# Seven products for eight in three more matrix products of a two-layer decoder trunk, with the middle of each layer reordered

## The chip, the cores and the metric

The kernel runs on one core of one Trainium2 chip. The metric is the device time of one execution in microseconds (us), the median of the runs taken. The program is one launch; the weights stay in HBM and stream through the core once per execution.

## The reference

Two layers over 256 tokens with a model width of 2048, all in f32. Each layer computes, in this order:

```
h = rmsnorm(x);  proj = h @ w_in      # columns: GLU pair, q, k, v, forget logits, gates A and B (2048 each)
y_conv = silu(layernorm(causal_depthwise_conv31(a * sigmoid(gate)))) @ w_conv_out
y_attn = forgetting_attention(q, k, v, cumsum(log_sigmoid(f))) @ w_attn_out     # 8 heads of 128
x += (sigmoid(g_A) * y_conv + sigmoid(g_B) * y_attn) @ w_out
x += (silu(gate) * up) @ w_down       # [gate | up] = rmsnorm(x) @ w_gate_up, hidden width 5632
x += sigmoid(rmsnorm(x) @ w_ple_gate) * (p[i] @ w_ple_proj)
```

At the end comes one more rmsnorm, which is the output.

## The kernel before, in words

Tokens sit in two blocks of 128. A product is done in chunks of 512 output columns: two PSUM banks, one for each token block, collect 16 tiles of 128 contraction rows. f32 exactness comes from splitting both operands into a high part (fp32r) and a rest, so that every (token block, row tile) pair costs three matmuls of 128x512 (L175 to L177): high by high, high by rest, rest by high. A chunk of 2048 rows is 96 of them.

Weights arrive as *raw* tiles of two row tiles by 512 columns (512 KB, L134, issued on SyncE's queue, 7 buffers in the pool `raws`). `split` (L137) makes the high part on ScalarE (L140) and the rest on VectorE (L141), into 4 buffers each (`whs`, `wls`); one split feeds 12 matmuls. Token operands are transposed on TensorE (L295, 8 transposes per 512 channels), evacuated by ScalarE, and the rest is subtracted on VectorE (`halves`, L279); they live in a pool of 23 buffers called `pairs`.

`fast_chunks` (L211) computes two chunks together. The first 4 row tiles by two token blocks by the two weight chunks are a 2x2 by 2x2 block product, done with seven block products for eight (a Winograd form): seven products of 6 matmuls, and 12 ordinary raw tiles (`go`) of 12 matmuls for the other 12 row tiles. For it VectorE adds weights (L241: one tile `sum`, three in place on `raw`), ScalarE copies one partial product out of PSUM (L254) and VectorE combines the rest (L255 to L258, L268 to L272). The seven products split seven tiles where the ordinary way splits four. Class `Fast` (L304) makes the token side: `take` evacuates the transposed first four tiles with the gains (L314) into two f32 tiles, `make` forms four more by subtracting (L320), and splits all eight (L329, L330). In this kernel its two f32 tiles are taken from `raws`. Only the FFN's gate and up products use `fast_chunks`, from their second pair of chunks on: ten pairs per layer.

Three lists steer what goes between chunks: `turns` (transposes of finished operands), `tasks` (attention, one step for each `run`), and `background` (the depthwise convolution's 248 VectorE steps and the layer norm after it, `fill(CONV)` with a credit of 7). `chunk` calls `run` and `fill` once per four row tiles. The framework then places each engine's instructions in an order that it plans from the order of the program and from which buffers are free; on the chip each engine works through its own list in that order.

In a layer the order is: GLU chunks (4), values (2), keys and queries (4, attention begins), gates A (4, the rest of the attention), gates B alternating with the attention's output product (`attended`, L786), the convolution's output product (L814) with the merge, the output projection `wOut` (L826), FFN in three parts, and the embeddings' gate `wPG` (L875) with the projection `wPP` (L866). `Norm(g_ffn, fast=True)` (L824) is the one norm per layer with a `Fast`; its `turn(0)` runs in the second chunk of `wOut`.

Of the kernel before, what the change touches and what calls it, by code (L numbers as in the profile page):

```python
# [10 lines left out]
F32 = mybir.dt.float32  # L11
# [5 lines left out]
P = 128  # L17
D = 2048
S = 256
# [25 lines left out]
def trunk(ctx, tc, xT, xR, pT, wI, wF, wC, wA, wOut, wGU, wD, wPG, wPP, vec, bF, gF, out):  # L45
# [162 lines left out]

    def fast_chunks(fast, w1, w2, xs, ks):  # L211


        nk = 4 * len(ks)
# [6 lines left out]
                for half in range(2):  # L221
                    left.append((w[1 + g][:, half * 1024 : (half + 1) * 1024], sums, k0 + 2 * half))

        def go(n=1):
            for _ in range(n):
                if left:
                    src, sums, k0 = left.popleft()
                    parts = split(fetch(src))
                    await_x(xs, (k0, k0 + 1))
                    plain(sums, xs, k0, parts)  # L230
                    if len(left) % 2 == 0:
                        run()
                        fill(CONV)

        def product(to, which, raw):
            h, l = split(raw)
# [36 lines left out]
        return (u1, u4), (u3, u5)  # L273

    def by_four(w, n=N4):
        return [(w[g], range(4 * g, 4 * g + 4)) for g in range(n)]
# [27 lines left out]
    class Fast:  # L304


        def __init__(self):
            self.f = [raws.tile([P, 4, 2, P], F32, tag="raw", name=f"fast{next(uid)}") for _ in range(2)]

        def take(self, half, pt, gains):  # L310
            src = pt.rearrange("p k (b s) -> p b k s", b=2)
            to = self.f[0][:, 2 * half : 2 * half + 2]
            for kk in range(2):
                act.activation(to[:, :, kk, :], src[:, :, kk, :], AF.Copy, scale=gains[kk])  # L314
            if half == 1:
                self.make()

# [27 lines left out]
                    lambda b, j=j, kk=kk: self.l[0][:, 2 * j + b, kk, :],  # L345
                )

    def operand(xs, k0, src):
        for half, pt in turned(src):
            o = pair(F32R)  # L350
            halves(o, pt)
            for kk in range(2):
                xs[k0 + 2 * half + kk] = by_blocks(o[:, kk, :])

    class Norm:

# [89 lines left out]
    def hook():  # L446
        load_x(0, 2, 4)
        take(0)

    def rest(q):  # L450
        def go():
            take(q)
            if q < 3:
                load_x(q + 1)
                turns.append(rest(q + 1))
            else:
                for b in range(2):
                    nc.sync.dma_start(xt[:, b, :], xR[:, b, :])
                nc.sync.dma_start(vecs[:, KD:], vec[:, KD:])
                nc.sync.dma_start(bfs, bF.rearrange("l h -> (l h)").partition_broadcast(P))  # L460
                for n in range(N4):
                    norm.squares(n)
                norm.finish()
        return go

    for i in range(L):
# [70 lines left out]

        def logits():
            pf = bank_ms()
            for k in range(KD):  # L540
                pe.matmul(
                    pf[:16, :], lhsT=wfc[:, k].rearrange("p a h -> p (a h)"), rhs=norm.tiles[k],
                    start=(k == 0), stop=(k == KD - 1),
                )
            act.activation(fls[:16, :], pf[:16, :], AF.Copy)

        def log_forget():
# [221 lines left out]

        background.append(lazy(conv_norm))  # L770

        gate_a, y_att = [], []

        def sigmoids(c):
            pp = project(c)
            t = pair()
            for b in range(2):
                act.activation(t[:, b, :], pp[b], AF.Sigmoid, scale=norm.r(b))
            return t

        for n in range(N4):
            gate_a.append(sigmoids(GATE_A + n))
        while tasks:
            run()

        def attended(n):  # L786
            return chunk(by_four(wA[i, n], 2), o_att, bank_mm)
# [5 lines left out]
        for n in range(N4 - 1):  # L793
            t = sigmoids(GATE_B + n)
            gated_by(t, attended(n))
            y_att.append(t)
        pp = attended(N4 - 1)
        t = pair()
        for b in range(2):
            act.activation(t[:, b, :], pp[b], AF.Copy)  # L800
        s = project(GATE_B + N4 - 1)
        for b in range(2):
            g = tmp()
            act.activation(g, s[b], AF.Sigmoid, scale=norm.r(b))
            dve.tensor_tensor(t[:, b, :], t[:, b, :], g, op=ALU.mult)
        y_att.append(t)
        while background:
            fill(9)


        merged = {}
        for n in range(N4):
            t = gate_a[n]
            gated_by(t, chunk(by_four(wC[i, n], 2), o_conv, bank_mm))  # L814
            for b in range(2):
                dve.tensor_tensor(t[:, b, :], t[:, b, :], y_att[n][:, b, :], op=ALU.add)
            turns.append(lambda n=n, t=t: operand(merged, 4 * n, lambda b: t[:, b, :]))

        def residual(n, acc):
            for b in range(2):  # L820
# [1 line left out]
                dve.tensor_tensor(xc, xc, acc[b], op=ALU.add)  # L822

        norm = Norm(g_ffn, fast=True)  # L824
        for n in range(N4):
            residual(n, chunk(by_four(wOut[i, n]), merged, bank_mm))  # L826
            advance(norm, n)


        after = Norm(g_ple)  # L830
        c0 = 0
        for part, nch in enumerate(FFN_PARTS):
            hid = {}
            for c in range(c0, c0 + nch):
                w1, w2 = wGU[i, 2 * c], wGU[i, 2 * c + 1]
                if c == 0:
                    g, t = [chunk(by_four(w), norm.xs, bank_mm) for w in (w1, w2)]
                    o = [tmp() for _ in range(2)]
                else:
                    g, t = fast_chunks(norm.fast, w1, w2, norm.xs, (4, 8, 12))  # L840
                    o = t
                for b in range(2):
                    z = tmp()
                    act.activation(z, g[b], AF.Sigmoid, scale=norm.r(b))
                    dve.scalar_tensor_tensor(z, g[b], norm.r(b), z, op0=ALU.mult, op1=ALU.mult)
                    dve.scalar_tensor_tensor(o[b], t[b], norm.r(b), z, op0=ALU.mult, op1=ALU.mult)
                turns.append(lambda c=c, o=o, hid=hid: operand(hid, 4 * c, lambda b: o[b]))
            for n in range(N4):
                groups = [(wD[i, n, c], range(4 * c, 4 * c + 4)) for c in range(c0, c0 + nch)]
                residual(n, chunk(groups, hid, bank_mm))  # L850
                if part == len(FFN_PARTS) - 1:
                    advance(after, n)
# [9 lines left out]

        last = i == L - 1

        def embed(n):
            return chunk([(wPP[i, n], range(2))], ps, bank_ms)  # L866
# [6 lines left out]
        for n in range(N4):  # L873
            e = embed(n)
            acc = chunk(by_four(wPG[i, n]), norm.xs, bank_mm)  # L875
            for b in range(2):
                t = tmp()
                act.activation(t, acc[b], AF.Sigmoid, scale=norm.r(b))
                dve.tensor_tensor(t, t, e[b], op=ALU.mult)
                xc = xt[:, b, n * 512 : (n + 1) * 512]  # L880
                dve.tensor_tensor(xc, xc, t, op=ALU.add)
            if not last:
                advance(after, n)
                continue
            after.squares(n)
            if n == N4 - 1:
                after.finish()
            for b in range(2):
                xc = xt[:, b, n * 512 : (n + 1) * 512]
                dve.tensor_tensor(xc, xc, gb[n // 2][:, (n % 2) * 512 : (n % 2 + 1) * 512], op=ALU.mult)  # L890
        norm = after


# [66 lines left out]
```

## Time and profile before

| | |
|---|---|
| median of 3 runs | 2891.67 us (2891.22 to 2892.88) |
| the profiled execution | 2891.74 us |
| its span in the trace | 2889.9 us |
| TensorE matmul busy | 2855.0 us, 12884 instructions |
| VectorE busy | 2001.4 us |
| ScalarE busy | 1431.1 us |
| mean granted TensorE clock | 0.996 |
| DMA | 543.27 MB, 188 GB/s |

Times in the trace run from the span's start. Busy time of TensorE is modelled from pipelined matmuls: one matmul lasts 390 ns in the records and the next begins 0.23 us after it, so work done is better read from how many matmuls a stretch holds. A wait is put down to what ended last before it.

### The profile page before, as it was taken

How to read it: one execution, taken by the hardware profiler on the slowest of the kernel's cores; microseconds unless marked ns; L12 is line 12 of the kernel's file. 1: busy time of each engine (PE TensorE's matmuls, PEld its weight loads, DVE VectorE, ACT ScalarE, POOL GpSimd, SP SyncE). 2: the span in 40 equal slices, each digit the busy share in tenths (PEclk: the TensorE clock that was granted, in tenths of full speed). 3: DMA queues.
4: the chain of work that ended last, by engine and by line, in shares of the span. 5: the costliest groups of instructions: out<-in, count | busy, mean ns of one | idle time of the engine just before them, and what ended most of it. 6: DMA issues, size and time to landing. Idle time of an engine off the chain costs nothing.

```text
span 2889.9 us, 34305 instructions
## 1 busy us (share of the span) xinstructions
PE 2855.0 (99%) x12884; PEld 2361.8 (82%) x12884; DVE 2001.4 (69%) x2568; ACT 1431.1 (50%) x1726; POOL 9.5 (0%) x40
## 2 busy tenths in 40 slices
PE   8999999999999999999999999999999999999998
PEld 6888888788888888888888888887888888888886
DVE  5997745557678758865569966455585886688554
ACT  5445744455445435545554456444454554455444
POOL 0000000000000000000000000000000000000000
PEclk9999999999999999999999999999999999999999
DMA  7554455455556556555555544554455555556553
GB/s 279 180 179 166 166 197 191 165 185 180 207 183 209 198 178 211 182 204 189 183 176 188 180 163 175 195 190 162 177 191 207 182 196 204 181 197 211 186 203 122
DMA packets 149496, 543.27 MB, mean 188 GB/s; under 512 B 16849, under 2 KB 17105, under 8 KB 149073
## 3 DMA queue, kind: packets, MB, share of 16 engines
q1 hardware_dynamic: 149328, 541.07, 54.1%
q8 instruction: 101, 1.65, 0.2%
q14 instruction: 67, 0.54, 0.1%
HBM read 538.91 MB, written 2.10 MB: 187 GB/s over the span
## 4 chain that ended last, share of the span: by engine, by line
PE 94%; DVE 4%; DMA 1%; ACT 0%; issue 0%; SPq 0%; POOL 0%; ACTq 0%; POOLq 0%; DVEq 0%
PE mm L176 29%; PE mm L177 29%; PE mm L175 29%; PE ms L295 2%; DVE wl L141 2%; DVE pair L490 2%; PE ms L177 2%; PE ms L176 2%; PE ms L175 2%; DMA xt<-in_xR_dram 0%; PE ms L649 0%; DMA raw<-in_wI_dram 0%; PE ms L685 0%; ACT tmp L368 0%; PE ms L651 0%
## 5 line engine op out<-in xcount | busy, mean ns | idle before, releaser
L141 DVE TENSOR_TENSOR wl<-raw,wh 128x1024 fp32r<-128x1024 f32 x1054 | 1282.3, 1223 | 802.1 <-ACT wh L140 793.8
L140 ACT ACTIVATE wh<-raw 128x1024 fp32r<-128x1024 f32 x1054 | 1116.3, 1060 | 1299.9 <-PE mm L177 1186.1
L175 PE MATMUL mm<-wh,pair 128*128 128x512 f32 x3832 | 1502.8, 392 | 18.6 <-ACT wh L140 11.1
L176 PE MATMUL mm<-wl,pair 128*128 128x512 f32 x3832 | 1495.7, 390 | 1.8 <-DVE wl L141 1.8
L177 PE MATMUL mm<-wh,pair 128*128 128x512 f32 x3832 | 1495.9, 390 | 0.0
L175 PEld LDWEIGHTS mm<-wh,pair 128*128 128x128 f32 x3832 | 721.1, 188 | 166.9 <-ACT wh L140 12.0
L176 PEld LDWEIGHTS mm<-wl,pair 128*128 128x128 f32 x3832 | 721.8, 188 | 151.7 <-DVE wl L141 3.4
L177 PEld LDWEIGHTS mm<-wh,pair 128*128 128x128 f32 x3832 | 721.4, 188 | 150.7
L490 DVE SCALAR_TENSOR_TENSOR pair<-pair,vecs,pair 128x256 f32<-128x256 f32 x480 | 201.3, 476 | 0.0
L177 PE MATMUL ms<-wh,pair 128*128 128x512 f32 x192 | 74.7, 389 | 0.0
L175 PE MATMUL ms<-wh,pair 128*128 128x512 f32 x192 | 74.7, 389 | 0.0
L176 PE MATMUL ms<-wl,pair 128*128 128x512 f32 x192 | 74.7, 389 | 0.0
L241 DVE TENSOR_TENSOR raw<-raw,raw 128x1024 f32<-128x1024 f32 x60 | 73.2, 1221 | 0.9
L283 DVE TENSOR_TENSOR pair<-ms,pair 128x512 fp32r<-128x512 f32 (+1 forms) x76 | 45.1, 625 | 1.6 <-ACT pair L282 1.3
L822 DVE TENSOR_TENSOR xt<-xt,mm 128x512 f32<-128x512 f32 x64 | 41.1, 680 | 4.9 <-PE mm L177 4.9
L175 PEld LDWEIGHTS ms<-wh,pair 128*128 128x128 f32 x192 | 36.0, 188 | 7.5
L176 PEld LDWEIGHTS ms<-wl,pair 128*128 128x128 f32 x192 | 36.0, 188 | 7.5
L177 PEld LDWEIGHTS ms<-wh,pair 128*128 128x128 f32 x192 | 36.0, 188 | 7.5
L368 ACT ACTIVATE tmp<-xt 128x512 f32<-128x512 f32 x56 | 34.6, 619 | 14.9 <-DVE xt L822 8.8
L282 ACT ACTIVATE pair<-ms 128x512 fp32r<-128x512 f32 (+1 forms) x76 | 38.0, 541 | 0.6 <-PE ms L686 0.6
L285 ACT ACTIVATE pair<-ms,vecs 128x256 fp32r<-128x256 f32 x72 | 30.6, 467 | 14.4 <-DVE pair L286 14.4
L140 ACT ACTIVATE wh<-sum 128x1024 fp32r<-128x1024 f32 x20 | 21.2, 1062 | 31.3 <-PE mm L177 31.3
(167 smaller groups left out, 925.3 us busy)
## 6 DMA issues: line engine op xcount, KB each, us to landing
raw<-in_wGU_dram SPq DMA_DIRECT2D x352, 512.0 KB, 4.1
raw<-in_wI_dram SPq DMA_DIRECT2D x287, 512.0 KB, 3.8
raw<-in_wD_dram SPq DMA_DIRECT2D x176, 512.0 KB, 3.7
raw<-in_wOut_dram SPq DMA_DIRECT2D x64, 512.0 KB, 3.7
raw<-in_wPG_dram SPq DMA_DIRECT2D x64, 512.0 KB, 3.6
raw<-in_wA_dram SPq DMA_DIRECT2D x32, 512.0 KB, 4.2
raw<-in_wC_dram SPq DMA_DIRECT2D x32, 512.0 KB, 4.3
raw<-in_wPP_dram SPq DMA_DIRECT2D x8, 512.0 KB, 3.2
```

The source lines that it names most:

```text
L140: act.activation(h, raw, AF.Copy)
L141: dve.tensor_tensor(l, raw, h.bitcast(F32), op=ALU.subtract)
L175: pe.matmul(self.t, lhsT=xh, rhs=wh, start=start, stop=False)
L176: pe.matmul(self.t, lhsT=xh, rhs=wl, start=False, stop=False)
L177: pe.matmul(self.t, lhsT=xl, rhs=wh, start=False, stop=self.left == 0)
L241: add = lambda o, a, b: dve.tensor_tensor(o, a, b, op=ALU.add)
L282: act.activation(hi, src, AF.Copy)
L283: dve.tensor_tensor(lo, src, hi.bitcast(F32), op=ALU.subtract)
L295: pe.transpose(pt[:, kk * S + b * P : kk * S + (b + 1) * P], src(b)[:, c : c + P], ident)
L368: act.activation(tmp(), xt[:, b, n * 512 : (n + 1) * 512], AF.Square, accum_out=self.ss[:, b * 4 + n : b * 4 + n + 1],)
L490: dve.scalar_tensor_tensor(cv[c], u[c][:, j : j + S], w, cv[c], op0=ALU.mult, op1=ALU.add,)
L822: dve.tensor_tensor(xc, xc, acc[b], op=ALU.add)
```

## The change

`fast_chunks` also computes the gates A and B (two pairs of chunks each per layer), the output projection (two pairs) and the embeddings' gate (two pairs). It gets a callback `first` for the first chunk's result, called half-way, and may write into given tiles (`to`). Gates B are all computed first, then the attention's output product, then a pair of gates A, two chunks of the convolution's output product, and the same once more. `Fast` takes its f32 tiles from `pairs`; there is one for the merged operand, one for each norm ahead of the embeddings and of layer 2, and one made from the first layer's input (`early`). In `go`, `run` is called after every raw tile but one, and the background credit of 7 is dealt in 3 and 4.

```diff
-    def fast_chunks(fast, w1, w2, xs, ks):
+    def fast_chunks(fast, w1, w2, xs, ks, first, to=None):
...
-        def go(n=1):
+        def go(n=1, quiet=False):
...
                     plain(sums, xs, k0, parts)
-                    if len(left) % 2 == 0:
+                    fill(CONV // 2 + len(left) % 2)
+                    if not quiet:
                         run()
-                        fill(CONV)
...
         product(q5, M1, a21)
-        go()
+        go(quiet=True)
         product(q7, T3, s3)
...
-        u1, u3, u4, u5 = (tmp() for _ in range(4))
+        u1, u4, u3, u5 = [tmp() for _ in range(4)] if to is None else to
...
         add(u4, u4, c12.t)
+        first((u1, u4))
         go(2 * len(ks))
...
-            self.f = [raws.tile([P, 4, 2, P], F32, tag="raw", name=f"fast{next(uid)}") for _ in range(2)]
+            self.f = [pair().rearrange("p a (n k s) -> p (a n) k s", n=2, k=2) for _ in range(2)]
...
+            if gains is None:
+                act.activation(to, src, AF.Copy)
...
+    def early():
+        norm.fast = Fast()
+        for j in range(2):
+            norm.fast.take(
+                j, xin[0][:, j, :].rearrange("p (k s) -> p k s", k=2), [norm.gain(2 * j + kk) for kk in range(2)]
+            )
+        norm.xs.update(enumerate(norm.fast.column_tiles()))
...
-            for k in range(KD):
...
+            for k in range(4, KD):
+                pe.matmul(pf[:16, :], lhsT=lhsT(k), rhs=norm.tiles[k], start=(k == 4), stop=False)
+            for k, (hi, lo) in enumerate(norm.fast.both()):
+                pe.matmul(pf[:16, :S], lhsT=lhsT(k), rhs=hi, start=False, stop=False)
+                pe.matmul(pf[:16, S:], lhsT=lhsT(k), rhs=lo, start=False, stop=(k == 3))
...
         def sigmoids(c):
-            pp = project(c)
...
+            t = [pair() for _ in range(2)]
+            def gate(t):
+                for b in range(2):
+                    act.activation(t[b], t[b], AF.Sigmoid, scale=norm.r(b))
+            gate(fast_chunks(
+                norm.fast, wI[i, c], wI[i, c + 1], norm.xs, (4, 8, 12), gate,
+                [t[m][:, b, :] for m in range(2) for b in range(2)],
+            ))
             return t
...
+        y_att = sigmoids(GATE_B) + sigmoids(GATE_B + 2)
         while tasks:
             run()
...
+        for n in range(N4):
+            gated_by(y_att[n], chunk(by_four(wA[i, n], 2), o_att, bank_mm))
...
         merged = {}
+        fast_merged = Fast()
         for n in range(N4):
-            t = gate_a[n]
+            if n % 2 == 0:
+                gate_a = sigmoids(GATE_A + n)
...
+            t = gate_a[n % 2]
             gated_by(t, chunk(by_four(wC[i, n], 2), o_conv, bank_mm))
...
+                lambda n=n, t=t: operand(merged, 4 * n, lambda b: t[:, b, :], fast_merged if n == 0 else None)
...
-            residual(n, chunk(by_four(wOut[i, n]), merged, bank_mm))
-            advance(norm, n)
...
+        for n in range(0, N4, 2):
+            onto_x(norm, n + 1)(
+                fast_chunks(fast_merged, wOut[i, n], wOut[i, n + 1], merged, (4, 8, 12), onto_x(norm, n))
+            )
...
-        after = Norm(g_ple)
+        after = Norm(g_ple, fast=True)
...
-        after = Norm(0 if last else (i + 1) * NV)
-        for n in range(N4):
-            e = embed(n)
-            acc = chunk(by_four(wPG[i, n]), norm.xs, bank_mm)
...
+        after = Norm(0 if last else (i + 1) * NV, fast=not last)
...
+        for n in range(0, N4, 2):
+            for m in range(2):
+                e.append(pair())
+                for b, t in enumerate(chunk([(wPP[i, n + m], range(2))], ps, bank_ms)):
+                    act.activation(e[n + m][:, b, :], t, AF.Copy)
+            embedded(n + 1)(
+                fast_chunks(norm.fast, wPG[i, n], wPG[i, n + 1], norm.xs, (4, 8, 12), embedded(n))
+            )
```

In the FFN the gate's silu moves into the callback, half-way through a pair; the sum for x in `embedded` is the residual, the square sums and, in the first layer, the next norm's `turn`.

## Rows read from the trace of the kernel before

**Rows 1.** The page's first part: busy us (share of the span) xinstructions.
```profile
PE 2855.0 (99%) x12884; PEld 2361.8 (82%) x12884; DVE 2001.4 (69%) x2568; ACT 1431.1 (50%) x1726; POOL 9.5 (0%) x40
```

**Rows 2.** The chain that ended last, share of the span by engine.
```profile
PE 94%; DVE 4%; DMA 1%; ACT 0%; issue 0%; SPq 0%; POOL 0%; ACTq 0%; POOLq 0%; DVEq 0%
```

**Rows 3.** Waits of TensorE: us in total, times, longest us.
```profile
PE mm L175 <- ACT wh L140: 11.1, 3, 4.4
PE mm L175 <- ACT wh L159: 7.5, 2, 6.8
PE mm L176 <- DVE wl L141: 1.8, 3, 0.8
```

**Rows 4.** Windows: a plain chunk of `wOut`, then two FFN pairs, one set of transposes each.
```profile
core 0: us, PE busy (x) PEld busy (x) DVE busy (x) ACT busy (x) POOL busy (x), PEclk, DMA share, GB/s
586.99:609.64 22.65, 22.65 (x106) 18.85 (x105) 12.66 (x14) 11.30 (x16) 0.00 (x0) 1.00 0.53 186
1136.08:1179.16 43.08, 43.08 (x196) 35.74 (x195) 35.72 (x38) 22.76 (x24) 0.00 (x0) 1.00 0.57 195
```

**Rows 5.** The chain by time: one set of transposes between two chunks of `wOut`.
```profile
586.99 0.87 PE ms L295 x8
```

**Rows 6.** Windows around the second chunk of `wOut`, layers 1 and 2, and within the latter.
```profile
555.00:575.00 20.00, 14.89 (x63) 11.82 (x62) 11.35 (x13) 10.65 (x13) 0.00 (x0) 0.91 0.58 193
1985.00:2005.00 20.00, 15.38 (x59) 11.85 (x57) 10.39 (x12) 9.59 (x12) 0.00 (x0) 0.83 0.49 167
1995.00:2000.00 5.00, 4.76 (x12) 3.63 (x12) 3.75 (x4) 1.73 (x2) 0.00 (x0) 0.50 0.81 261
```

**Rows 7.** ScalarE's instructions in time there, layer 1: start, us, what, idle before.
```profile
546.47 1.06 ACT L140 ACTIVATE wh<-raw 128x1024 fp32r<-128x1024 f32 x1 [1.66 <-PE mm L177]
...
557.79 1.57 ACT L314 ACTIVATE fast<-ms,vecs 128x256 f32<-128x256 f32 x4 [4.44 <-PE ms L295]
559.40 2.19 ACT L329 ACTIVATE pair<-fast 128x1024 fp32r<-128x1024 f32 x2
561.49 3.88 ACT L140 ACTIVATE wh<-raw 128x1024 fp32r<-128x1024 f32 x4
```

**Rows 8.** SyncE's weight transfers there, in time.
```profile
528.89 0.33 SPq L134 DMA_DIRECT2D raw<-in_wOut_dram  x1
537.05 0.33 SPq L134 DMA_DIRECT2D raw<-in_wOut_dram  x1
...
548.82 0.33 SPq L134 DMA_DIRECT2D raw<-in_wOut_dram  x1
561.74 0.33 SPq L134 DMA_DIRECT2D raw<-in_wOut_dram  x1
```

**Rows 9.** Groups by line, engine and form: xcount | busy us, mean ns | idle before.
```profile
L141 DVE TENSOR_TENSOR wl<-raw,wh 128x1024 fp32r<-128x1024 f32 x1054 | 1282.3, 1223 | 802.1 <-ACT wh L140 793.8 <-DMA wf<-in_wF_dram 1.5 <-DMA raw<-in_wI_dram 0.7
L241 DVE TENSOR_TENSOR raw<-raw,raw 128x1024 f32<-128x1024 f32 x60 | 73.2, 1221 | 0.9
L255 DVE TENSOR_TENSOR tmp<-tmp,ms 128x512 f32<-128x512 f32 x20 | 13.6, 680 | 0.0
L541 PE MATMUL ms<-pair,wfc 128*16 128x512 f32 x32 | 7.9, 399 | 0.0
L656 PE MATMUL ms<-chs,nsel 128*128 128x256 f32 x16 | 4.5, 279 | 0.0
```

**Rows 10.** Windows: convolution under keys and queries; gates A with attention; the second GLU chunk.
```profile
180.00:240.00 60.00, 59.94 (x290) 49.93 (x289) 60.00 (x126) 29.55 (x43) 0.00 (x0) 1.00 0.49 174
252.00:348.00 96.00, 95.73 (x455) 79.64 (x455) 64.28 (x123) 64.19 (x100) 0.70 (x1) 1.00 0.44 154
...
40.00:60.00 20.00, 20.00 (x90) 16.57 (x89) 9.94 (x9) 9.34 (x10) 0.00 (x0) 1.00 0.68 231
```

**Rows 11.** The end of the trace: the last matmul, and VectorE's first instruction behind it.
```profile
2875.98 0.39 PE L177 MATMUL mm<-wh,pair 128*128 128x512 f32 x1
2876.45 1.37 DVE L879 TENSOR_TENSOR tmp<-tmp,ms 128x512 f32<-128x512 f32 x2 [8.60 <-ACT tmp L878]
```

More of the change, by code (lines that the diff above doesn't have):

```diff
@@ L346, in column_tiles, with both, operand @@
                 )
-    def operand(xs, k0, src):
+        def both(self):
+            for k in range(4):
+                j, kk = divmod(k, 2)
+                yield self.h[0][:, 2 * j : 2 * j + 2, kk, :], self.l[0][:, 2 * j : 2 * j + 2, kk, :]
+    def operand(xs, k0, src, fast=None):
         for half, pt in turned(src):
+            if fast is not None:
+                fast.take(half, pt)
+                continue
             o = pair(F32R)
@@ L353, in operand @@
                 xs[k0 + 2 * half + kk] = by_blocks(o[:, kk, :])
+        if fast is not None:
+            xs.update(zip(range(k0, k0 + 4), fast.column_tiles()))
     class Norm:
@@ L456, in go @@
             else:
+                turns.append(early)
                 for b in range(2):
@@ L539, in logits @@
             pf = bank_ms()
-            for k in range(KD):
[L541 to L544, printed above, removed]
+            lhsT = lambda k: wfc[:, k].rearrange("p a h -> p (a h)")
+            for k in range(4, KD):
[3 more added lines that the diff above has]
+                pe.matmul(pf[:16, S:], lhsT=lhsT(k), rhs=lo, start=False, stop=(k == 3))
             act.activation(fls[:16, :], pf[:16, :], AF.Copy)
@@ L791, in gated_by @@
                 dve.tensor_tensor(t[:, b, :], t[:, b, :], pp[b], op=ALU.mult)
[L793 to L808, printed above, removed]
+        y_att = sigmoids(GATE_B) + sigmoids(GATE_B + 2)
+        while tasks:
+            run()
+        for n in range(N4):
+            gated_by(y_att[n], chunk(by_four(wA[i, n], 2), o_att, bank_mm))
         merged = {}
+        fast_merged = Fast()
         for n in range(N4):
-            t = gate_a[n]
+            if n % 2 == 0:
+                gate_a = sigmoids(GATE_A + n)
+            if n == 0:
+                while background:
+                    fill(9)
+            t = gate_a[n % 2]
             gated_by(t, chunk(by_four(wC[i, n], 2), o_conv, bank_mm))
@@ L816, in trunk @@
                 dve.tensor_tensor(t[:, b, :], t[:, b, :], y_att[n][:, b, :], op=ALU.add)
-            turns.append(lambda n=n, t=t: operand(merged, 4 * n, lambda b: t[:, b, :]))
+            turns.append(
+                lambda n=n, t=t: operand(merged, 4 * n, lambda b: t[:, b, :], fast_merged if n == 0 else None)
+            )
         def residual(n, acc):
@@ L824, in trunk, with onto_x, go @@
         norm = Norm(g_ffn, fast=True)
-        for n in range(N4):
-            residual(n, chunk(by_four(wOut[i, n]), merged, bank_mm))
-            advance(norm, n)
-        after = Norm(g_ple)
+        def onto_x(norm, n):
+            def go(y):
+                residual(n, y)
+                if norm is not None:
+                    advance(norm, n)
+            return go
+        for n in range(0, N4, 2):
[3 more added lines that the diff above has]
+        after = Norm(g_ple, fast=True)
         c0 = 0
@@ L835, in trunk, with gate @@
                 w1, w2 = wGU[i, 2 * c], wGU[i, 2 * c + 1]
+                z = [tmp() for _ in range(2)]
+                def gate(g, z=z):
+                    for b in range(2):
+                        act.activation(z[b], g[b], AF.Sigmoid, scale=norm.r(b))
+                        dve.scalar_tensor_tensor(z[b], g[b], norm.r(b), z[b], op0=ALU.mult, op1=ALU.mult)
                 if c == 0:
[L837 to L841 removed]
+                    gate(chunk(by_four(w1), norm.xs, bank_mm))
+                    up = chunk(by_four(w2), norm.xs, bank_mm)
+                else:
+                    up = fast_chunks(norm.fast, w1, w2, norm.xs, (4, 8, 12), gate)
                 for b in range(2):
[L843 to L846, printed above, removed]
+                    dve.scalar_tensor_tensor(z[b], up[b], norm.r(b), z[b], op0=ALU.mult, op1=ALU.mult)
+                o = z
                 turns.append(lambda c=c, o=o, hid=hid: operand(hid, 4 * c, lambda b: o[b]))
@@ L849, in trunk @@
                 groups = [(wD[i, n, c], range(4 * c, 4 * c + 4)) for c in range(c0, c0 + nch)]
-                residual(n, chunk(groups, hid, bank_mm))
-                if part == len(FFN_PARTS) - 1:
-                    advance(after, n)
+                onto_x(after if part == len(FFN_PARTS) - 1 else None, n)(chunk(groups, hid, bank_mm))
             c0 += nch
@@ L863, in trunk @@
         last = i == L - 1
-        def embed(n):
-            return chunk([(wPP[i, n], range(2))], ps, bank_ms)
         if last:
@@ L871, in trunk, with embedded, go @@
                 nc.sync.dma_start(gb[n], gF[n * 1024 : (n + 1) * 1024].partition_broadcast(P))
-        after = Norm(0 if last else (i + 1) * NV)
-        for n in range(N4):
-            e = embed(n)
-            acc = chunk(by_four(wPG[i, n]), norm.xs, bank_mm)
[L876 to L890, printed above, removed]
+        after = Norm(0 if last else (i + 1) * NV, fast=not last)
+        e = []
+        def embedded(n):
+            def go(y):
+                for b in range(2):
+                    act.activation(y[b], y[b], AF.Sigmoid, scale=norm.r(b))
+                    dve.tensor_tensor(y[b], y[b], e[n][:, b, :], op=ALU.mult)
+                residual(n, y)
+                if not last:
+                    advance(after, n)
+                    return
+                after.squares(n)
+                if n == N4 - 1:
+                    after.finish()
+                for b in range(2):
+                    xc = xt[:, b, n * 512 : (n + 1) * 512]
+                    dve.tensor_tensor(xc, xc, gb[n // 2][:, (n % 2) * 512 : (n % 2 + 1) * 512], op=ALU.mult)
+            return go
+        for n in range(0, N4, 2):
[5 more added lines that the diff above has]
+                fast_chunks(norm.fast, wPG[i, n], wPG[i, n + 1], norm.xs, (4, 8, 12), embedded(n))
+            )
         norm = after
```

18 lines of the change are left out of this document (5 added, 13 removed).

## The prediction

> **What bounds the kernel now.** I read the page first: TensorE is busy 2855.0 of 2889.9 us, VectorE 2001.4 and ScalarE 1431.1 [rows 1]. The chain of waits agrees: 94% of it is TensorE, 4% VectorE, 1% DMA [rows 2]. The reader is to see that nothing but TensorE's own work sets the time in most stages, so that a matmul less is time less as long as its operands come in time. Then TensorE's waits, to see where they don't: it waits for the high part of a weight split three times (11.1 us, longest 4.4), for the very first weights (7.5), and for the rest part 1.8 us [rows 3]. The windows around these waits come last; two of the three stand in the second chunk of `wOut`, one in each layer [rows 6].
>
> **The price of a pair, and what goes.** A plain chunk of `wOut` takes 22.65 us between two sets of transposes, an FFN pair in the seven-product form 43.08 [rows 4]; a set of 8 transposes is 0.87 [rows 5]. So a plain pair is 2 x (22.65 - 0.87) = 43.56, a fast pair 43.08 - 0.87 = 42.21, and the form saves 1.35 us. The count says the same: 192 matmuls become 12 x 12 + 7 x 6 = 186, and six at 21.78/96 = 0.227 are 1.36. There are 4 + 2 + 2 new pairs per layer and two layers, so 16 x 1.35 = 21.6 us go from TensorE, which is the path.
>
> The TensorE page of the Trainium skill ("TensorE: Matmul & The Clock Gate", Back-to-back issue gap) gives about 131 ns as the sustained spacing of such matmuls in a real kernel and 216 ns in isolation. By the first the 96 matmuls would be an estimated 12.6 us, by the second 20.7; the 0.227 us here lies beside the second, and no stretch of this trace shows the first.
>
> **The stall in `wOut`.** SyncE issues a weight transfer about every 2.7 us (3.6 across transposes), but none between 528.89 and 537.05, and then none between 548.82 and 561.74 [rows 8]. The first gap is as wide as two buffers: the `Fast` tiles of the coming norm have taken two of the seven `raws`. ScalarE makes its last split at 546.47, then stands for 4.44 us at the evacuation of the transposes (L314), makes the operand (2.19), and only then does four splits in one go [rows 7]: with five buffers the planned order put those splits behind the operand, though the weights had long been there. TensorE ran dry meanwhile, and came back at a lower clock (0.50 granted in the 5 us from 1995) [rows 6]. The price: the window from 555 holds 63 records, 8 of them transposes, so 55 x 0.227 + 0.87 = 13.4 us of work in 20, 6.6 lost; that from 1985 holds 59, so 12.4 of work, 7.6 lost. Together 14.2; idle time alone would be 5.1 + 4.6 = 9.7. I take 14.2, since the lower clock is lost work too. The change takes the `Fast` tiles from `pairs`, so all seven buffers serve the weights, and I expect the splits to be planned ahead as in the other chunks. If they aren't, 14.2 stay. After these two, no TensorE wait of over a microsecond is left beyond the start.
>
> **What is added on VectorE and ScalarE.** A fast pair has 3 more splits (1.223 each), 4 additions (1.221) and 8 half-size combinations (0.680) on VectorE [rows 9]: 3.67 + 4.88 + 5.44 = 14.0 us per pair; ScalarE gets 3 splits and a copy, under 4 us against a load of half its time [rows 1]. The FFN pairs show the result where little else runs: 35.72 us of VectorE in 43.08, with TensorE never idle [rows 4]. In `wOut` and the embeddings' gate the residual (4 x 0.680), the gating and the next operand stand in place of the silu; 19 splits, 4 additions and 16 to 24 steps of 0.680 or less are 39 to 45 us, with two splits of `wPP` in the embeddings' pair 47, against 43 and 49 of TensorE (24 matmuls of `wPP`, 5.4 us). So these are covered: cost nothing, and if a pair's cover went, up to 2 us each.
>
> The tight place is the first two pairs, gates B, under which the rest of the attention and the convolution's layer norm run. The stage that they replace, four plain chunks, has 64.28 us of VectorE in 96.00 [rows 10]. With 2 x 14.0 it is 92.3 against 96.0 - 2.7 = 93.3 of TensorE. The credit per pair falls from 56 to 42, so the eight closing steps of the layer norm (four VectorE operations each, half as wide as the 0.680 ones) slide under the attention's output product, where plain chunks leave VectorE nearly half free (12.66 of 22.65) [rows 4]; that leaves between 92.3 and 92.3 - 32 x 0.68 = 70.5. Full load alone does no harm: under keys and queries VectorE is busy 60.00 of 60 and TensorE still 59.94 [rows 10], because four split buffers let it run up to 4 x 2.72 = 10.9 us ahead. But a pair's first half is heavier: 11 splits, 4 additions and 4 combinations are 21.0 us against 90 matmuls, 20.4. I put 1.2 us of new waits in each layer, 2.5 in all; the bounds are 0 (the 59.94) and 18 (third rival). That gates A come later, after the attention, costs nothing by itself: their weights come through the same queue in the same number (16 transfers per pair), and the only thing that waits for them is the convolution's merge, which moved behind them too.
>
> Both ends of the small terms. Logits: 16 wide matmuls become 12 wide and 8 of half width; half width lasts 279 ns against 399 [rows 9], so between nothing (half the price) and +0.9 per layer (full price); I take 0.25, 0.5 in all, nearer the first because columns set the pace. `early` puts 4 evacuations, 2 splits and 6 VectorE steps, about 4 us on each engine, beside a plain chunk in which both are half idle (9.34 and 9.94 of 20) [rows 10]: nothing, or 4 if they fall ahead of a split. Could it win? Only if it moved the start's 7.5 us wait, which it comes after. The end: behind the last matmul VectorE now first subtracts (0.68) before the sigmoid, where ScalarE read PSUM directly; the second block's subtraction runs under it. The chain behind 2875.98 [rows 11] grows by 0.7 to 1.4; I take 0.8. Silu at half-way in the FFN moves work off the pair's end, where nothing waited: 0. The doubled pace of `run` halves the gap between a head's scores and its transposes from four splits' matmuls to two (5.4 us); the softmax between must fit into that, and what it lacks is in the 2.5.
>
> **Sum**, against the profiled execution's own 2891.74 (span 2889.9 and 1.84 around it; the median of the runs is 2891.67, 0.07 away): 2891.74 - 21.6 - 14.2 + 2.5 + 0.5 + 0.8 = 2859.7. I forecast **2860**; with every addition at nothing 2856, and some 2 less if `early` eases the start; with 8 us of waits in place of 2.5, 2866.
>
> **Rivals.**
> *The stall stays in `wOut` (2874).* 2860 + 14.2, if the evacuation itself and not the buffers holds the splits back. For it: ScalarE does wait there for TensorE's transposes. Against it: the other turns, with seven buffers, show no such wait, and the gap at 528.89 has no other cause in the program.
>
> *VectorE sets the pace in gates B (2878).* With no lead left, the first half of such a pair needs 21.0 us of its own and 0.26 per us for the stage's other VectorE work ((64.28 - 32 splits of 1.223)/96) [rows 9, 10]. TensorE takes 20.4 x 96/87.1 = 22.5 us for it with the attention's matmuls (87.1 are four plain chunks). So VectorE lacks 21.0 + 5.9 - 22.5 = 4.4 us; four such pairs in the program are 18. It decides where VectorE enters a pair with less than 4.4 us of lead. The lead of up to 10.9 speaks against it.
>
> *Slower: every new `Fast` brings the stall with it (2910).* If the long hold of ScalarE is the cause (4.44 of waiting, 1.57 and 2.19 of work [rows 7]), then each `Fast` fed by transposes costs it. There will be seven: two for the merged operand, two ahead of the FFN, two ahead of the embeddings, one ahead of layer 2. At 7.1 each they cost 49.7 where two cost 14.2 now: 2860 + 49.7. The kernel is slower once one costs over (2891.7 - 2860)/7 = 4.5 us. For it: the hold of 8.2 us is three quarters of what four split buffers cover; against it: splits can be planned ahead of the hold, which needs only raw buffers.
>
> The same page of the Trainium skill (Architectural detail) says that ScalarE and VectorE queues are strict first-in first-out, so a waiting evacuation holds every split behind it. The trace agrees: four splits start together at 561.49. That rule speaks for the two rivals with the hold, and is why I leave them more than a remnant.
>
> **Chances.** Forecast 0.58 (2853 to 2868), stall stays 0.15, gates B bound 0.15, slower 0.12. About 0.2% (5.8 us) is what a measurement of this kernel can tell. The first two are faster by more; gates B bound is so in three parts of five, the rest within 0.2%: faster 0.82, same 0.06, slower 0.12. The range 2853 to 2882 holds the first two and the better part of the third, 0.8.
>
> **What would show it.** Right: 96 fewer wide matmuls (11,976 in place of 12,072); fast pairs of 42.2 us plus transposes in all new places; in `wOut` no gap of SyncE over 6 us, no burst of four splits behind L329, and a granted clock of 1.00. Wrong: TensorE waits for the rest part (VectorE) inside the gates B pairs (third case); waits for the high part behind each `take` (slower); a stall of about 7 us in `wOut` alone (second). The forecast also falls if the `pairs` pool, with four more tiles for each `Fast`, holds an operand back: then TensorE would wait for transposed operands, which it does nowhere now.

## The result: 2863.26 us, 1.0% less, and the profile after

The changed kernel takes 2863.26 us (median of 4, 2861.74 to 2863.95) beside 2892.28 for the kernel before, measured beside it; the ratio is 0.9899, 95% interval 0.9882 to 0.9916. The forecast was 2860. The profiled execution took 2863.95, its span is 2862.1, so 27.8 us less than the 2889.9 of before.

The first part of its page (busy us, share, instructions), to be held beside [rows 1]:

```profile
PE 2831.8 (99%) x12796; PEld 2342.3 (82%) x12796; DVE 2208.6 (77%) x2828; ACT 1502.5 (52%) x1814; POOL 9.5 (0%) x40
```

TensorE's instructions are 88 fewer: the products have 96 wide matmuls less, and the logits 8 wide ones less and 16 of half width more. VectorE has 207 us more to do. The wide matmuls themselves, by group (xcount | busy us, mean ns | idle before):

```profile
L175 PE MATMUL mm<-wh,pair 128*128 128x512 f32 x3672 | 1439.4, 392 | 12.7 <-ACT wh L159 7.6
L175 PE MATMUL ms<-wh,pair 128*128 128x512 f32 x320 | 125.6, 393 | 2.1 <-ACT pair L922 2.1
```

3 x (3672 + 320) = 11,976, as forecast; one still lasts 392 ns in the records. TensorE's waits (us in total, times, longest), beside [rows 3]:

```profile
PE mm L175 <- ACT wh L159: 7.6, 1, 7.6
PE mm L175 <- ACT wh L140: 5.1, 4, 3.3
PE ms L175 <- ACT pair L922: 2.1, 3, 1.1
PE mm L176 <- DVE wl L141: 0.4, 1, 0.4
```

The two waits of 4.4 us are gone. Of the four for L140 that are left, the longest (3.3) stands at the start, at 30.37 us, where the kernel before has one too; the other three (0.3, 1.2 and 0.3) stand in the embeddings. A new kind, for L922, has come: the evacuation of `wPP`'s chunk. To see where the time went, sets of transposes serve as milestones, since both kernels have the same ones. These are from the chain by time (start us, us, what), first of the kernel before, then after:

```profile
65.44 0.87 PE ms L295 x8
182.06 0.87 PE ms L295 x8
682.15 0.87 PE ms L295 x8
1327.89 0.87 PE ms L295 x8
1452.37 0.87 PE ms L295 x8
1613.42 0.87 PE ms L295 x8
```

```profile
66.95 0.87 PE ms L297 x8
183.61 0.87 PE ms L297 x8
668.98 0.87 PE ms L297 x8
1314.71 0.88 PE ms L297 x8
1440.79 0.87 PE ms L297 x8
1601.82 0.87 PE ms L297 x8
```

The stretches between them, with the FFN's milestones of layer 2 (2114.61 and 2760.34 before, 2087.18 and 2732.91 after) and the last matmul (2875.98 before, 2847.21 after). In the column of the forecast 8.1 is six pairs, 2.7 two pairs, 6.6 and 7.6 are the stall, and 1.2 the new waits:

| stretch | before | after | change | forecast |
|---|---|---|---|---|
| start to first transposes | 65.44 | 66.95 | +1.5 | 0 |
| to the keys, with the logits | 116.62 | 116.66 | 0.0 | +0.25 |
| keys to FFN, layer 1 | 500.09 | 485.37 | -14.7 | -8.1 - 6.6 + 1.2 |
| FFN, layer 1 | 645.74 | 645.73 | 0.0 | 0 |
| embeddings, layer 1 | 124.48 | 126.08 | +1.6 | -2.7 |
| to the keys, layer 2 | 161.05 | 161.03 | 0.0 | +0.25 |
| keys to FFN, layer 2 | 501.19 | 485.36 | -15.8 | -8.1 - 7.6 + 1.2 |
| FFN, layer 2 | 645.73 | 645.73 | 0.0 | 0 |
| embeddings, layer 2, to the last matmul | 115.64 | 114.30 | -1.3 | -2.7 |
| behind the last matmul | 13.92 | 14.89 | +1.0 | +0.8 |

The embeddings are the one stage where the pairs did not pay: 4.3 and 1.4 us of the forecast gain are missing. In `wOut` there is no stall any more. ScalarE's splits stand there one at a time, no four in a row behind L334 (L329 in the kernel before), and the longest gap of SyncE over the place of the stall is 5.93 us (from 552.18), where it was 12.92. One of 6.38, over the 6 us that the forecast named as its sign, stands at 508.28, and TensorE waits nowhere near it. Windows over the second chunk's place (us, busy of PE, PEld, DVE, ACT, POOL, clock, DMA share, GB/s), where [rows 6] had clocks of 0.91 and 0.83:

```profile
540.00:600.00 60.00, 60.00 (x279) 49.95 (x278) 51.92 (x59) 36.70 (x50) 0.00 (x0) 1.00 0.60 207
1980.00:2040.00 60.00, 60.00 (x278) 49.94 (x278) 47.53 (x56) 34.49 (x48) 0.69 (x1) 1.00 0.59 199
```

### The profile page after: what moved, and what is told of

The parts are those of the page before. It is cut to its first block, busy times and chain, and to the rows that moved or that the text cites. A ratio compares the mean times of both kernels' runs of the same rounds, so it can differ in the third digit from the quotient of the medians.

```text
span 2862.1 us, 34502 instructions
## 1 busy us (share of the span) xinstructions
PE 2831.8 (99%) x12796; PEld 2342.3 (82%) x12796; DVE 2208.6 (77%) x2828; ACT 1502.5 (52%) x1814; POOL 9.5 (0%) x40
## 4 chain that ended last, share of the span: by engine, by line
PE 92%; DVE 5%; ACT 1%; DMA 1%; issue 1%; SPq 0%; ACTq 0%; POOLq 0%; POOL 0%; DVEq 0%
PE mm L176 27%; PE mm L177 27%; PE mm L175 27%; PE ms L175 2%; PE ms L176 2%; PE ms L177 2%; DVE wl L141 2%; PE ms L297 2%; DVE pair L514 2%; DMA pair<-in_xT_dram 0%; PE ms L674 0%; DMA raw<-in_wI_dram 0%; ACT tmp L383 0%; ACT wh L140 0%; PE ms L710 0%
## 5 line engine op out<-in xcount | busy, mean ns | idle before, releaser
L140 ACT ACTIVATE wh<-raw 128x1024 fp32r<-128x1024 f32 x1086 | 1152.3, 1062 | 1215.9 <-PE mm L177 1048.4
L141 DVE TENSOR_TENSOR wl<-raw,wh 128x1024 fp32r<-128x1024 f32 x1086 | 1320.7, 1224 | 596.2 <-ACT wh L140 583.8
L175 PE MATMUL mm<-wh,pair 128*128 128x512 f32 x3672 | 1439.4, 392 | 12.7 <-ACT wh L159 7.6
L176 PE MATMUL mm<-wl,pair 128*128 128x512 f32 x3672 | 1432.7, 390 | 0.6 <-DVE wl L141 0.4
L177 PE MATMUL mm<-wh,pair 128*128 128x512 f32 x3672 | 1432.3, 390 | 0.0
L175 PEld LDWEIGHTS mm<-wh,pair 128*128 128x128 f32 x3672 | 690.6, 188 | 154.1 <-ACT wh L159 7.6
L177 PEld LDWEIGHTS mm<-wh,pair 128*128 128x128 f32 x3672 | 690.6, 188 | 144.2
L242 DVE TENSOR_TENSOR raw<-raw,raw 128x1024 f32<-128x1024 f32 x108 | 131.9, 1221 | 1.5
L175 PE MATMUL ms<-wh,pair 128*128 128x512 f32 x320 | 125.6, 393 | 2.1 <-ACT pair L922 2.1
L177 PE MATMUL ms<-wh,pair 128*128 128x512 f32 x320 | 124.6, 389 | 0.0
L176 PE MATMUL ms<-wl,pair 128*128 128x512 f32 x320 | 124.6, 389 | 0.0
L175 PEld LDWEIGHTS ms<-wh,pair 128*128 128x128 f32 x320 | 60.1, 188 | 15.5 <-ACT pair L922 3.2
L177 PEld LDWEIGHTS ms<-wh,pair 128*128 128x128 f32 x320 | 60.1, 188 | 12.6
L140 ACT ACTIVATE wh<-sum 128x1024 fp32r<-128x1024 f32 x36 | 38.2, 1062 | 46.5 <-PE mm L177 46.5
L141 DVE TENSOR_TENSOR wl<-sum,wh 128x1024 fp32r<-128x1024 f32 x36 | 44.0, 1222 | 13.4 <-ACT wh L140 13.4
L242 DVE TENSOR_TENSOR sum<-raw,raw 128x1024 f32<-128x1024 f32 x36 | 44.0, 1222 | 0.6
```

The costliest lines, as they stand in the source:

```text
L140: act.activation(h, raw, AF.Copy)
L141: dve.tensor_tensor(l, raw, h.bitcast(F32), op=ALU.subtract)
L175: pe.matmul(self.t, lhsT=xh, rhs=wh, start=start, stop=False)
L176: pe.matmul(self.t, lhsT=xh, rhs=wl, start=False, stop=False)
L177: pe.matmul(self.t, lhsT=xl, rhs=wh, start=False, stop=self.left == 0)
L242: add = lambda o, a, b: dve.tensor_tensor(o, a, b, op=ALU.add)
```

## Experiments

Changes are given against the kernel named. Spans and milestones are of each one's profiled execution. The changed kernel came to 2863.26 above and to 2862.42 when it was measured again, so a difference of a microsecond between kernels that were not measured together says nothing; where kernels are alike, the stretches between milestones behind the start agree from trace to trace within some 0.1 us.

**What caused the stall in `wOut`: two kernels.** One line of the kernel before changed, and the same line of the changed kernel changed back:

```diff
-            self.f = [raws.tile([P, 4, 2, P], F32, tag="raw", name=f"fast{next(uid)}") for _ in range(2)]
+            self.f = [pair().rearrange("p a (n k s) -> p (a n) k s", n=2, k=2) for _ in range(2)]
```

> The kernel before, with one line changed: Fast's two f32 tiles from the pool of pairs instead of raws. Theory (buffers): the stall in wOut came from two of seven weight buffers being taken; it goes in both layers, about 14.2 us: 2878, and the windows around the second chunk of wOut show TensorE busy throughout at clock 1.00. Rival (the long hold of ScalarE at the evacuation): nothing changes, 2892 within 2.

Measured 2877.12 (2876.78 to 2878.00), ratio 0.9949 (0.9933 to 0.9966): 15.0 us less by this line alone. The two windows in its trace:

```profile
540.00:600.00 60.00, 60.00 (x275) 49.85 (x274) 35.17 (x38) 31.03 (x44) 0.00 (x0) 1.00 0.55 185
1980.00:2040.00 60.00, 60.00 (x279) 49.94 (x278) 35.17 (x40) 31.39 (x44) 0.00 (x0) 1.00 0.55 185
```

TensorE is never idle there. ScalarE's list at the same place, beside [rows 7]:

```profile
546.42 1.06 ACT L140 ACTIVATE wh<-raw 128x1024 fp32r<-128x1024 f32 x1 [1.66 <-PE mm L177]
549.14 1.06 ACT L140 ACTIVATE wh<-raw 128x1024 fp32r<-128x1024 f32 x1 [1.66 <-PE mm L177]
551.86 1.06 ACT L140 ACTIVATE wh<-raw 128x1024 fp32r<-128x1024 f32 x1 [1.66 <-PE mm L177]
...
554.91 1.06 ACT L140 ACTIVATE wh<-raw 128x1024 fp32r<-128x1024 f32 x1 [0.76 <-ACT tmp L368]
557.36 1.06 ACT L140 ACTIVATE wh<-raw 128x1024 fp32r<-128x1024 f32 x1 [1.39 <-PE mm L177]
558.32 1.55 ACT L314 ACTIVATE pair<-ms,vecs 128x256 f32<-128x256 f32 x4
559.90 1.06 ACT L329 ACTIVATE pair<-pair 128x1024 fp32r<-128x1024 f32 x1
560.91 1.06 ACT L140 ACTIVATE wh<-raw 128x1024 fp32r<-128x1024 f32 x1
561.88 1.04 ACT L329 ACTIVATE pair<-pair 128x1024 fp32r<-128x1024 f32 x1
```

Four splits now stand between 546.42 and the evacuation, and one between the two L329; the evacuation itself waits for nothing, since ScalarE comes to it later. From keys to FFN its layers take 493.08 (182.01 to 675.09) and 493.09 (1606.37 to 2099.46), 7.0 and 8.1 less than before. SyncE's longest gap between 500 and 640 us is 3.73 us here; the gaps of 8.16 and 12.92 [rows 8] are gone.

> The changed kernel with Fast's two f32 tiles taken from raws again. Theory (buffers): stalls come back; at least in wOut (2863 + 14 = 2877), at most behind all seven Fasts that are fed by transposes, 7 x 7.1 = 50 (2913); more Fasts than two show a gap of SyncE and a burst of splits. Rival (hold): 2863 within 2.

Measured 2918.44 (2917.74 to 2918.67), ratio 1.0091 (1.0076 to 1.0106): 55 us more than the changed kernel, 7.9 for each of the seven. TensorE's waits in it:

```profile
PE mm L175 <- ACT wh L140: 33.3, 11, 4.5
PE mm L175 <- ACT wh L159: 7.7, 2, 7.5
```

Seven more waits for the high part than the four after, longest 4.5 us: the stall of the kernel before, once for each `Fast` fed by transposes. The milestones say the same: keys to FFN, with two of them per layer, take 501.05 and 502.03, 15.7 and 16.7 more than after. ScalarE's evacuation is the same in all these kernels; only the pool differs that the two tiles come from. So the buffers were the cause; the hold alone, with seven buffers, costs nothing.

**The embeddings' waits: three kernels.** The chunks of `wPP` use two banks each of the pool `ms`, which has four. In the changed kernel ScalarE's list between the FFN and the embeddings is (start, us, what, idle before):

```profile
1334.73 1.06 ACT L140 ACTIVATE wh<-raw 128x1024 fp32r<-128x1024 f32 x1 [0.44 <-ACT tmp L383]
1335.70 0.82 ACT L287 ACTIVATE pair<-ms,vecs 128x256 fp32r<-128x256 f32 x2
1336.41 1.08 ACT L922 ACTIVATE pair<-ms 128x512 f32<-128x512 f32 x2
1337.48 0.87 ACT L287 ACTIVATE pair<-ms,vecs 128x256 fp32r<-128x256 f32 x2
```

and TensorE's, which waits for L140, then for L922:

```profile
1334.48 1.04 PE L297 MATMUL ms<-ident,xt 128*128 128x128 f32 x8
1335.84 0.73 PE L175 MATMUL mm<-wh,pair 128*128 128x512 f32 x2 [0.32 <-ACT wh L140]
1337.06 0.50 PE L175 MATMUL ms<-wh,pair 128*128 128x512 f32 x1 [0.48 <-ACT pair L922]
```

The transposes of the norm's last operand hold two banks and the first `wPP` chunk the other two; the second chunk can only begin when ScalarE has emptied one. The same waits come back, longer, between the two pairs of layer 1, and VectorE is full there (4.00 of 4 us) while the granted clock stays at 1.00:

```profile
1386.79 0.73 PE L175 MATMUL mm<-wh,pair 128*128 128x512 f32 x2 [1.20 <-ACT wh L140]
1389.53 0.50 PE L175 MATMUL ms<-wh,pair 128*128 128x512 f32 x1 [1.11 <-ACT pair L922]
1382.00:1386.00 4.00, 3.59 (x16) 2.63 (x14) 4.00 (x6) 2.61 (x4) 0.00 (x0) 1.00 0.34 116
1386.00:1390.00 4.00, 2.10 (x12) 1.64 (x13) 4.00 (x6) 3.78 (x9) 0.00 (x0) 1.00 0.09 24
```

First, one chunk moved to the other pool:

```diff
-                for b, t in enumerate(chunk([(wPP[i, n + m], range(2))], ps, bank_ms)):
+                for b, t in enumerate(chunk([(wPP[i, n + m], range(2))], ps, bank_ms if m else bank_mm)):
```

> The changed kernel, with the first of each two chunks of wPP in a bank of the mm pool instead of ms. Milestones in the two traces put 4.3 us of new waits into layer 1's embeddings and 1.4 into layer 2's. Theory (banks): the four ms banks hold the last operand's two transposes and the first wPP chunk, and the second chunk waits for their evacuation; with the first in mm 4 to 5.5 us go: 2858 to 2859. Rival (VectorE and ScalarE are simply full there, whatever the banks): 2863 within 1.

Measured 2859.41 (2858.00 to 2860.10), ratio 0.9886 (0.9872 to 0.9901), 3.9 us under the changed kernel. The waits for L922 are gone:

```profile
PE mm L175 <- ACT wh L159: 7.3, 1, 7.3
PE mm L175 <- ACT wh L140: 5.6, 2, 4.4
```

Layer 1's embeddings take 123.62 (1313.45 to 1437.07), 1.8 more than the 121.8 that the pairs should give: a wait of 1.20 us for a split between the two pairs is left (the wait of 4.4 in the list is the start's). By the milestones 2.5 us come back in layer 1 and 1.1 in layer 2 (113.22), of 5.7. Then the part undone, with the embeddings as before and no `Fast` ahead of them:

```diff
-            embedded(n + 1)(
-                fast_chunks(norm.fast, wPG[i, n], wPG[i, n + 1], norm.xs, (4, 8, 12), embedded(n))
-            )
...
+            e = chunk([(wPP[i, n], range(2))], ps, bank_ms)
+            acc = chunk(by_four(wPG[i, n]), norm.xs, bank_mm)
...
```

> The changed kernel with the embeddings' gate as in the kernel before (plain chunks, the projection read from PSUM, no Fast ahead of it). Theory (the new waits of 4.3 and 1.4 us eat the four pairs' 5.4): 2862 to 2864, no change. Rival (the waits come from the next norm's Fast, which stays): 2868.

Measured 2862.73 (2861.62 to 2863.10), ratio 0.9898: the embeddings' change bought nothing, as the first theory says. Its two stretches take 124.45 and 115.63, as in the kernel before, so the `Fast` of the next norm, which stays, costs nothing. Last, the second pair's `wPP` chunks half-way through the first pair, and the very first in `mm`:

```diff
+            def first(y, n=n):
+                embedded(n)(y)
+                if n == 0:
+                    embeds(2)
+
+            embedded(n + 1)(fast_chunks(norm.fast, wPG[i, n], wPG[i, n + 1], norm.xs, (4, 8, 12), first))
```

> The changed kernel with the wPP chunks of the second pair computed half-way through the first pair (in its callback), and the very first one in a bank of mm. Theory (banks and the crowd between two pairs): all of the 4.3 and 1.4 us of new waits in the embeddings go: 2857 to 2858. Rival (only the banks matter, and the rest of the loss is the pair's own): 2859.4, as with the bank alone.

Measured 2858.01 (2857.50 to 2858.78), ratio 0.9879 (0.9863 to 0.9896), 4.4 us under the changed kernel measured beside it:

> The changed kernel once more, beside the two below: 2863. The start (first set of transposes) scatters between 64.9 and 67.0 us over the traces so far, so single spans differ by up to 2 us; both theories say no more than that.

That one came to 2862.42 (2862.11 to 2863.62), ratio 0.9895. With the callback layer 1's embeddings take 122.34 (1313.43 to 1435.77), within 0.6 of the full gain, layer 2's 113.42, within 0.5, and TensorE is busy throughout:

```profile
1320.00:1380.00 60.00, 59.99 (x271) 48.88 (x271) 49.19 (x55) 38.97 (x54) 0.69 (x1) 1.00 0.54 175
1380.00:1440.00 60.00, 60.00 (x278) 49.65 (x277) 49.38 (x63) 37.95 (x56) 1.16 (x9) 1.00 0.63 203
```

So the loss was the crowd at the start of a pair, the banks the larger part of it (3.5 of the 4.6 us that came back). Where the last 1.0 went is open. No version measured was faster by more than 0.1 us.

**The start.** `early` tied to the first GLU chunk by its gains (added and subtracted, which leaves them as they are but for rounding):

```diff
+        dve.tensor_scalar(g, vecs[:, :4], early.dep, early.dep, op0=ALU.add, op1=ALU.subtract)
...
-                turns.append(early)
...
+                early.dep = at[1][:, 0:1]
+                turns.append(early)
```

> The changed kernel, with early made to depend on the evacuated first GLU chunk, so that it can't be planned before it. Theory: the start is 1.5 us later than in the kernel before because early's four evacuations (1.7 us) stand on ScalarE ahead of the square sums and the first splits; behind the chunk they are covered: 2861.7. Rival (early's work costs the same wherever it stands): 2863 within 0.7.

Measured 2862.65 (2862.35 to 2863.02), between the two. The same on top of the version with the callback:

> The same with early behind the first GLU chunk as well. Theory (early's cost at the start is 0.3 to 1.5 us): 0.3 to 1.5 less than the kernel without it. Rival (the start scatters for other reasons and early is covered): the same within 0.3.

Measured 2857.95 (2857.29 to 2858.13) beside 2858.01: no difference. The traces leave more open. In the ten with `early` as it was, the first transposes come between 64.92 and 66.95 us, at 66.2 on average, and the changed kernel measured again has 66.78; in the four with `early` later or absent they come between 65.37 and 65.51. So the start scatters by 2 us with `early` in it, and may be some 0.7 later on average, but the medians show no cost. The theory of 1.5 us falls; what the scatter comes from is not shown.

**VectorE in the gates: four kernels.** Is the gates' form limited by VectorE? First, the gates plain in the new order:

```diff
+            for m in range(2):
+                pp = project(c + m)
                 for b in range(2):
-                    act.activation(t[b], t[b], AF.Sigmoid, scale=norm.r(b))
-
-            gate(fast_chunks(
-                norm.fast, wI[i, c], wI[i, c + 1], norm.xs, (4, 8, 12), gate,
-                [t[m][:, b, :] for m in range(2) for b in range(2)],
-            ))
+                    act.activation(t[m][:, b, :], pp[b], AF.Sigmoid, scale=norm.r(b))
```

> The changed kernel with the gates A and B as plain chunks again, in the new order of the middle. Theory (the form saves 1.35 us per pair and the reordering nothing): eight pairs of gates, 10.8: 2874. Rival (VectorE gives the gates' gain back in part): 2863 to 2870.

Measured 2872.64 (2872.44 to 2873.58), ratio 0.9933 (0.9918 to 0.9948): 9.4 us over the changed kernel for 10.8 by the count. From keys to FFN layer 1 takes 490.36 (183.30 to 673.66) against 485.37, so 5.0 of 5.4 us are gained there. Then VectorE was loaded, with `extra` at 8 for each pair of gates B, in the pair's first half:

```diff
+        for _ in range(extra):
+            dve.tensor_tensor(u4, u4, u4, op=ALU.max)
```

> The changed kernel with 8 added VectorE operations (128x512, a maximum of a tile with itself, which changes nothing) in the first half of each of the four gates B pairs: 16 per layer, 9.8 to 10.9 us. Theory (lead): the stage from 240 to 360 us has VectorE busy 100.2 of 120, so this fits: 2863 to 2865. Rival (VectorE sets the pace in gates B already): all 20 us are added, 2883.

Measured 2876.15 (2875.84 to 2877.07): 12.9 us over the changed kernel, for 20 of added work (32 operations that last 0.68 us in the records, the next operation beginning after 0.60). Neither theory: not covered, not all of it paid. Windows of 4 us inside the second gates pair, and the matmul that waited (3.13 us for L141):

```profile
316.00:320.00 4.00, 4.00 (x21) 3.27 (x20) 4.00 (x8) 1.86 (x3) 0.00 (x0) 1.00 0.58 208
320.00:324.00 4.00, 3.06 (x18) 2.56 (x16) 4.00 (x11) 1.31 (x3) 0.00 (x0) 1.00 0.05 18
324.00:328.00 4.00, 1.81 (x4) 1.49 (x5) 4.00 (x10) 1.76 (x5) 0.00 (x0) 0.69 0.00 0
328.00:332.00 4.00, 4.00 (x11) 3.08 (x10) 3.88 (x9) 2.46 (x4) 0.00 (x0) 0.50 0.56 176
```

VectorE is full (4.00 of 4), TensorE runs dry, and for some microseconds afterwards works at half the clock: 11 matmuls in the last window where 4 us hold 17 or 18. They begin 0.43 us apart there:

```profile
328.49 0.63 PE L175 MATMUL mm<-wh,pair 128*128 128x512 f32 x1
328.91 0.63 PE L176 MATMUL mm<-wl,pair 128*128 128x512 f32 x1
```

With 24 operations in each pair:

> The same with 24 in each pair: 48 per layer, 29 to 33 us. Theory (lead): about 20 us of slack and up to 10.9 of lead per layer take it or nearly: 2863 to 2880, with TensorE waiting for the rest part inside these pairs. Rival (VectorE sets the pace already): 2923.

Measured 2901.66 (2898.11 to 2902.14), ratio 1.0032 (1.0020 to 1.0044): 38.4 over, for about 60 added. So about two thirds of what is added shows from the first operations on. The stage had 20 us of idle VectorE per layer by the windows, but not where it would help.

The 8 operations again, half-way through the pair:

> The changed kernel with the same 8 added VectorE operations per gates B pair, put half-way through the pair, behind the first chunk's sums, instead of in its first half, where they cost 13 us. Theory (a pair's first half is where VectorE is full and the lead is used up; the second half has room): 2863 to 2866. Rival (VectorE's sum over the stage is what counts): 2876 again.

Measured 2868.82 (2868.15 to 2869.54), ratio 0.9924 (0.9907 to 0.9940): 5.6 over, less than half of the first half's 12.9, but not nothing. The wait moved into the next pair:

```profile
280.00:300.00 20.00, 20.00 (x101) 16.75 (x100) 19.89 (x42) 13.74 (x21) 0.00 (x0) 1.00 0.29 97
320.00:340.00 20.00, 18.23 (x84) 14.76 (x84) 19.38 (x34) 13.64 (x22) 0.00 (x0) 1.00 0.65 211
```

VectorE is full in the second half of the first pair (19.89 of 20), and TensorE is dry for 1.8 us in the second pair. That the second pair begins without its lead is a reading; what the trace shows there is a wait of 1.32 us at 327.32 for the high part. ScalarE begins no split between 315.57 and 326.21: steps of the attention's softmax stand ahead of the splits in its list and wait for VectorE (L691 for L690, 0.94 and 1.36). So where in a pair the work stands counts, and VectorE's delay reaches TensorE through ScalarE too.

## Why the prediction was right, step by step

**The 21.6 us of matmuls.** The count was right (11,976), and so was the price where operands came in time: without the stall (the kernel before with the one line) keys to FFN is 493.08 and 493.09, in the changed kernel 485.37 and 485.36, so 7.7 per layer for six pairs' 8.1.

**The stall, 14.2.** Right in cause and size: 15.0 by the median, 7.0 and 8.1 by the milestones. Counting matmuls in a window, which takes the half-clock work along, came nearer than the idle time (9.7). What pointed to the cause was the gap of SyncE at 528.89 [rows 8], as wide as two buffers, before any hold on ScalarE. One reading was short: the hold was put at 8.2 us, from the wait for the transposes on. But ScalarE makes no split from 546.47 to 561.49, 15.0 us, more than the 10.9 that four split buffers cover; in the first part of it ScalarE waits for VectorE's sum ahead of the square sums:

```profile
551.96 0.63 ACT L368 ACTIVATE tmp<-xt 128x512 f32<-128x512 f32 x1 [4.42 <-DVE xt L822]
```

With all seven buffers four splits stand in this stretch ahead of the evacuation, and TensorE never waits.

**New waits, 2.5 in gates B.** 0.4 per layer were paid, 0.8 in all, and by the kernel with plain gates it is in the gates, A or B. But the reason that I gave, a lead of 10.9 us that would absorb it, was too generous: 8 operations more in a pair, some 5 us, already cost 12.9 in the program. What kept the waits small is more likely the price: I added durations from the records, and these overlap. Back to back, a split or an addition of 1.22 us is followed by the next operation after 1.14 (305.10, 306.24, 307.37 in the last kernel's trace), a combination of 0.69 after 0.60 (313.05, 313.65). By that a pair's first half is 15 x 1.14 + 4 x 0.60 = 19.5 us of VectorE, not 21.0, against 20.4 of TensorE; VectorE's busy time grew by 207 us in all, where 16 x 14.0 would be 224. The third rival had the mechanism in the main right (a pair's first half fills VectorE, though work in the second half cost 5.6 too) and overstated its size; the kernel stands on the good side of that edge, by less than the 5 us added.

**The embeddings, nothing.** This step failed: I counted VectorE's work there (47 us against 49) and found cover, and did not count banks, nor the stretch between two pairs, in which VectorE is full for 8 us although the pair's average is covered. The prediction did name a price if the cover went, up to 2 us a pair; 5.7 us were lost in four pairs, more than the 5.4 that they save. The pool `ms` was full where a pair begins. Over the whole program, the profiled execution is 4.25 us above the sum (2863.95 against 2859.7): 5.7 here, 1.5 at the start, 0.2 at the end, less 1.7 in the gates, 0.9 in the stall and 0.5 in the logits. So that the total came this near to 2860 is partly luck: a term put at nothing was more than half made up for by others put too high.

**The small terms.** Logits cost 0.0, not 0.5; the end grew by 1.0 for 0.8; `early` shows no cost in the medians, as forecast.

**Rivals.** *The stall stays*: refuted by the one-line kernel. *Every new `Fast` brings the stall*: its price was right (7.9 for each where I put 7.1, 2918 where I put 2910), its cause wrong; it needs the two buffers taken, as the changed kernel with tiles from `raws` shows. The strict order of ScalarE's queue, of which the Trainium skill tells ("TensorE: Matmul & The Clock Gate", Architectural detail), holds in both; the trace agrees in that four splits stood behind the evacuation [rows 7], but with seven buffers the plan puts splits in front of it, and the rule costs nothing.

## What to carry to other kernels

A stall at one place that has siblings without a stall is best explained by what the one has and the others lack; here two tiles borrowed from the prefetch pool cost 15 us at two places, and would have cost 55 at seven. When a transformation trades TensorE's work for VectorE's, average load says little: count the load of the heaviest stretch of a few microseconds, and the buffers and PSUM banks that two neighbouring pieces need at once. Milestones common to both traces show which stage kept its gain.

## What had not been expected

The cost of a short stall can be well above its idle time. In the changed kernel with tiles from `raws`, seven waits of 3.9 to 4.5 us cost 7.9 each. In the loaded kernel a wait of 3.13 us was followed by a granted clock of 0.50 over the window from 328 to 332, the lower of the two levels (1.2 against 2.4 GHz), and matmuls began 0.43 us apart instead of 0.227. And the first 65 us scatter by 2 us from one trace to the next among kernels that are alike up to there, so a difference of 1.5 us there, read from one pair of traces, says little.
